# Products on halves of the TensorE array queued side by side in fours and eights, with the mixer's task order set anew

## The chip, the core and the metric

The kernel runs on one core of a Trainium2 chip. The metric is the device time of one execution in microseconds (us). TensorE (PE in the profile) multiplies, with its weight loads shown apart as PEld; VectorE (DVE), ScalarE (ACT) and GpSimd (POOL) do elementwise work, and DMAs are issued mostly from SyncE's queue (SP), a few from ScalarE's.

## The reference, cut to what matters

One decoder layer on 512 tokens with D = 1024, in float32: a feed-forward block, a mixer, a second feed-forward block, each with norms and a residual. The mixer adds three branches: native sparse attention (compressed, selected and window branches), a gated delta rule, and cross-attention into 256 memory tokens. The two parts that the change touches most are the compression of keys and values and the products of values with probabilities:

```python
def compress_blocks(kv, pos_emb, w1, w2):       # for k and for v
    blocks = jnp.concatenate([ch[:, j:j + n_cmp] for j in range(r)], axis=2) + pos_emb[:, None, :]
    flat = blocks.transpose(0, 1, 3, 2, 4).reshape(b, n_cmp, g, CMP_BLOCK * dh)
    return jax.nn.silu(flat @ w1) @ w2          # w1: 2048 x 256

# selected and window branch: 8 heads in 2 groups of 4, head dimension 64
logits = jnp.einsum('bqgjd,bkgd->bgjqk', qb, kb) * NSA_HEAD_DIM ** -0.5 + bias
p = masked_softmax(logits, mask)
return jnp.einsum('bgjqk,bkgd->bqgjd', p.astype(vb.dtype), vb)
```

## The kernel before, in words

Float32 products are made of three products of high and low parts (`mm3`: high by high at L117, low by high or high by low at L118 and L119). A weight tile of 128 x 512 is loaded by SyncE into `wraw` (a ring of 4 buffers), ScalarE copies its high part `whi` (L106), and VectorE, or for some tasks GpSimd, makes its low part `wlo` (L109); each feeds 12 products. The program runs in stages: norm and FFN1, the mixer's projections with the delta rule, attention with the merge of the branches, the output projection, FFN2.

Within a stage the order of work is set by lists of task names in the table `PRM` (`order` for the projections and the delta rule, `order2` for attention and merge, `order0` and `order3` for the stages around them). A scheduler takes the instructions in that order; `off` gives a task a priority that lets its instructions go ahead of earlier tasks, and `pool` says which share of a task's low parts GpSimd makes. Each engine then runs its own list strictly in order. The tasks that the text names:

- `c` is a convolution of the delta rule (`dn_conv`): 24 products into one PSUM bank, then VectorE makes `cacc` from that bank (L217 and three steps at L635), after which the bank can be written again. `z` is the projection to the output gate (`ptm`, 96 products of 512 columns), `M10` a merge tile with products in `pfm`.
- `b0`, `b1` (`dn_subst`) invert 16 x 16 blocks for heads 0 and 1, and 2 and 3: VectorE's substitution (L742, L744) ends in a copy (L745), the result goes to DRAM (`dD`, by ScalarE's queue) and comes back as `Dc` (L749, by SyncE's queue). `e0`, `e1` (`dn_double`, L762) expand `Dc` by a mask into `Dm` and `DT`: three of the four on VectorE, one on GpSimd. The levels `d` (`pt`, L784) then need `Dm`.
- `p0` to `p7` (`cmp_hid`) are the chunks of the compression. A chunk has 4 products of 64 weight columns on 256 columns: two `k` for the keys in the left half of the array's columns (output partitions 0 to 63) and for the values in the right half (64 to 127), all into one bank `phid`. Their weights are two 256 KB tiles `w1` from the ring `wraw`. Being plain float32, a product shows as 2 records.
- `S` (`nsa_soft`) makes scores (`ps`, L1042) and probabilities `Pm`, `P` (`nsa_pt`) their 10 transposes (`ppt`, L1062) and copies to `PT` (L1065: the first two of a tile by VectorE, the third by ScalarE), `V` (`nsa_pv`) the products of values and `PT` (`po`, L1074). There are 8 tasks `V`, one for each pair of heads and branch; each has 8 products with 64 weight columns, over 512, 384, 256 and 128 columns, for group 0 on the left half and for group 1 on the right half of the array. `A` is cross-attention's softmax (`pms` L1083, `pmt` L1097).

Of the kernel before, what the change touches and what calls it, by code (L numbers as in the profile page):

```python
# [10 lines left out]
F32 = mybir.dt.float32  # L11
# [6 lines left out]
P = 128  # L18
# [18 lines left out]
PRM = {'order': ['i', 'a', 'w', 'c01', 'h01', 'r0', 'c00', 'c10', 'c02', 'l0', 'h00', 'h02', 'c12', 'k0', 'h10', 'c22', 'c11', 'h12', 'h11', 'h22', 'r1', 'k1', 'l1', 'b0', 'c21', 'z', 'h21', 'e0', 'c20', 'r2', 'h20', 'c32', 'l2', 'c31', 'd00', 'h31', 'k2', 'r3', 'd01', 'l3', 'b1', 'd02', 'x0', 's00', 'e1', 'd10', 'c30', 'h32', 'x1', 'd11', 'h30', 's01', 's02', 's03', 'q0', 'q3', 'p0', 'o0', 'p1', 'p2', 'p3', 'k3', 'd12', 's10', 'p4', 'q1', 'p5', 's11', 'p6', 'p7', 's12', 's13', 'o1', 'q2', 'f'], 'dma': {'l': 'sync', 'b': 'sync', 'd': 'scalar', 'c': 'sync', 'r': 'sync'}, 'off': {'b0': 300, 'h31': 400, 'r1': 50, 'h32': 50, 'h11': 200, 'h12': 200, 'd10': 100, 'A01': 100, 'A10': 100, 'A11': 100, 'A20': 400, 'A31': 100, 'A21': 20, 'x0': 20, 'x1': 20, 'L': 200, 'S310': 400, 'S001': 20, 'S311': 400, 'A30': 100, 'r0': 400, 'd02': 20, 's11': 100, 'V20': 400, 'l3': 100, 'q1': 20, 'f': 400, 'l1': 20, 'h20': 100, 'h22': 100, 'r3': 50, 'P010': 50, 'y': 100, 'h02': 50, 'S101': 20, 'A00': 100, 'Q0': 50, 'Q1': 200, 'Q2': 50, 'Q3': 50, 'P110': 400, 'V31': 50, 'd01': 200, 'o0': 400, 'p0': 50, 'p1': 50, 'p2': 50, 'p4': 50, 'p5': 20, 'p6': 50, 'p7': 50, 'b1': 200, 'h01': 100, 'M15': 20, 'P201': 400, 'e0': 100, 'e1': 100, 'o1': 20, 'q0': 50, 'q2': 20, 'h21': 20, 'd11': 50, 'p3': 50, 'U0': 100, 's13': 50, 'c11': 20, 's00': 200, 'P011': 400, 'M14': 200, 'c20': 50, 'k2': 20, 'M03': 20}, 'ph': 'e', 'po': 'ss', 'xpd': (0, 1, 2), 'order2': ['K1', 'K0', 'B', 'M10', 'Q0', 'C0', 'Q1', 'S000', 'C3', 'S001', 'P001', 'P000', 'C1', 'S010', 'C2', 'S011', 'V00', 'P010', 'Q2', 'S101', 'S100', 'P011', 'S110', 'V01', 'P100', 'W0', 'P101', 'S111', 'Q3', 'V10', 'P110', 'M12', 'S200', 'P111', 'V11', 'P200', 'S210', 'M14', 'S201', 'M15', 'P201', 'S211', 'W1', 'V20', 'P211', 'P210', 'V21', 'S301', 'S300', 'W2', 'P301', 'S311', 'M11', 'P300', 'L', 'M13', 'S310', 'G0', 'V30', 'P310', 'M16', 'G2', 'P311', 'M17', 'V31', 'W3', 'A00', 'M00', 'A01', 'G1', 'U0', 'M05', 'A10', 'A11', 'G3', 'A30', 'U1', 'A31', 'U3', 'M03', 'M06', 'A20', 'A21', 'U2', 'M07', 'M22', 'M20', 'M02', 'M24', 'M27', 'M21', 'M23', 'M01', 'M04', 'M26', 'M25'], 'order0': ['d0', 'p0', 'n0', 't0', 'd1', 'k2', 'k0', 'p2', 'p3', 'v', 'k3', 'n1', 'k1', 't1'], 'order3': ['s3', 's7', 's2', 's6', 's1', 's5', 's0', 's4', 'd00', 'd01', 'd11', 'g', 'p0', 'n0', 't0', 'd10', 'p1', 'n1'], 't3': (('mm', 'r'), ('e', 's')), 'pool': {'W2': 2, 's13': 3, 'k0': 0, 'k1': 0, 'k2': 0, 'k3': 2, 'p3': 1, 'C0': 1, 'C1': 0, 'C2': 0, 'C3': 2, 'S310': 0, 'L': 3, 'd11': 3, 'p0': 1, 'p1': 1, 'p2': 1, 'p4': 2, 'p5': 1, 'p6': 1, 'p7': 1, 'S311': 0, 'h01': 0, 'h00': 2, 'h02': 0, 'h10': 0, 'h11': 0, 'h12': 0, 'h22': 0, 'h21': 0, 'h20': 0, 'h31': 0, 'h30': 3, 'h32': 0, 'i': 2, 'P011': 2, 'c21': 0, 'd01': 2, 'S000': 0, 'S001': 0, 'S010': 0, 'S011': 0, 'S100': 0, 'S101': 0, 'S110': 0, 'S111': 0, 'S200': 0, 'S201': 0, 'S210': 0, 'S211': 0, 'S300': 0, 'S301': 0, 'M24': 2, 'G2': 2, 'A01': 0, 'M10': 1, 'M15': 2, 'M12': 2, 'M14': 2, 'M13': 2, 'M17': 2, 'M11': 2, 'M16': 2, 'M23': 0, 'M27': 3, 'M01': 2, 'M00': 2, 'M03': 0, 'M07': 2, 'M06': 1, 'M22': 2, 'M04': 2, 'M20': 2, 'M26': 3, 'M02': 0, 'M21': 2, 'M25': 2, 'M05': 2, 'c11': 1, 'o1': 3, 'P000': 2, 'P001': 1, 'P010': 2, 'P100': 2, 'P101': 2, 'P110': 2, 'P111': 2, 'P200': 2, 'P201': 2, 'P210': 2, 'P211': 2, 'P301': 0, 'P300': 2, 'P310': 2, 'P311': 2, 'c12': 0, 'b1': 1, 'x0': 0, 'x1': 0, 'V21': 0, 'c30': 0, 'c01': 0, 'c02': 0, 'c00': 0, 'c10': 0, 'c22': 0, 'c20': 0, 'c31': 0, 'c32': 0, 's01': 3, 'A31': 0, 'd12': 0, 'y': 2, 'G0': 2, 'G1': 2, 'G3': 0, 'U3': 0, 'W3': 2, 'r1': 2, 's12': 3, 'U2': 0, 'Q0': 2, 'Q1': 2, 'Q2': 2, 'Q3': 1, 's00': 3, 's02': 2, 's03': 3, 's10': 2, 's11': 3, 'e1': 2, 'd00': 1, 'U0': 0, 'U1': 0, 'l2': 0, 'd02': 2, 'K1': 3, 'V11': 0, 'V00': 2}, 'pool3': {'d00': 3, 'd01': 3, 'd10': 3, 'd11': 0, 'p1': 2, 't1': 3, 't0': 3, 's5': 2, 's7': 2, 's1': 2, 's0': 2, 's3': 2, 's6': 2, 's2': 2, 's4': 2, 'q0': 1}, 'pool0': {}, 'off0': {'p3': 20, 'n1': 50, 'd0': 200, 'k2': 400, 'k1': 400}, 'off3': {'s1': 20, 's5': 200, 'g': 200, 't0': 400, 'd10': 200, 'p0': 200}, 'tt': ('e', 's'), 'order_s': ['t00', 'w10', 'w00', 'y', 't01', 't02', 'w01', 't03', 'w11', 'R0', 'F000', 'x', 'F101', 'n', 'F200', 't10', 't11', 't12', 't13', 'c', 'F110', 'B', 'F211', 'F011'], 't0': ('e', 's'), 'rs': ((0, 0), (0, 0)), 'ra': (1, 1), 'warm': 8, 'pools': {'F000': 0, 'F101': 0, 'F200': 0, 'F011': 0, 'F110': 0, 'F211': 0, 'w10': 0, 'w11': 0, 't00': 0, 't01': 0, 't02': 0, 't03': 0, 't13': 0, 't10': 0, 't11': 0, 't12': 0, 'w00': 0, 'w01': 0}, 'ptc': 'vvs', 'cva': 'v', 'offs': {'t13': 100, 'R1': 400, 't03': 20, 'w10': 200}, 'vnc': 's', 'sp3': 0, 'hsc': 'vv', 'sf2': 2, 'psc': 'vvvv', 'sp1': 0, 'vbs': 'v', 't1c': 'vs', 'sgv': 256}  # L37


class Body:  # L40
# [172 lines left out]
    def scale(self, eng, out, src, r):  # L213
        if eng == "s":
            self.nc.scalar.activation(out, src, AF.Copy, scale=r)
        else:
            (self.nc.gpsimd if eng == "g" else self.nc.vector).tensor_scalar(out, src, r, None, op0=OP.mult)  # L217
# [709 lines left out]
    def cmp_hid(self, c, Xs, d):  # L927
# [4 lines left out]
        w1 = []  # L932
        for which in range(2):
            w = self.wp.tile([P, 2, 256], F32, tag="wraw", name="w1", bufs=self.WB[0])
            nc.sync.dma_start(w, self.a["cmp_w1"][which, c])
            w1.append(w)
        for k in range(2):
            m = 2 * c + k
            for which in range(2):
                nc.tensor.matmul(d["ph"][64 * which : 64 * which + 64], Xs[which][:, m].rearrange("p g c -> p (g c)"),  # L940
                                 w1[which][:, k], start=m == 0, stop=m == 15)
# [574 lines left out]
```

## Time and profile before

| what | value |
|---|---|
| median of 3 runs | 1361.38 us (1360.89 to 1362.07) |
| the profiled execution | 1360.6 us |
| its span, first to last instruction | 1358.8 us |
| PE busy | 1330.2 us, 98% |
| DVE, ACT, POOL busy | 899.9, 717.7, 142.3 us |
| mean granted TensorE clock | 0.995 |
| DMA | 178.32 MB, mean 131 GB/s |

All times of rows are in us from the span's start, of this one execution. A row of the timeline begins with the start, then the time from its first start to its last end, the engine, the line, the operation and the tiles; xN is the number of records in the row. A span of consecutive matmuls ends a little after the next row starts, since matmuls are pipelined.

### The profile page before, as it was taken

How to read it: one execution, taken by the hardware profiler on the slowest of the kernel's cores; microseconds unless marked ns; L12 is line 12 of the kernel's file. 1: busy time of each engine (PE TensorE's matmuls, PEld its weight loads, DVE VectorE, ACT ScalarE, POOL GpSimd, SP SyncE). 2: the span in 40 equal slices, each digit the busy share in tenths (PEclk: the TensorE clock that was granted, in tenths of full speed). 3: DMA queues.
4: the chain of work that ended last, by engine and by line, in shares of the span. 5: the costliest groups of instructions: out<-in, count | busy, mean ns of one | idle time of the engine just before them, and what ended most of it. 6: DMA issues, size and time to landing. Idle time of an engine off the chain costs nothing.

```text
span 1358.8 us, 21802 instructions
## 1 busy us (share of the span) xinstructions
PE 1330.2 (98%) x7839; PEld 1128.1 (83%) x7839; DVE 899.9 (66%) x1802; ACT 717.7 (53%) x1538; POOL 142.3 (10%) x129
## 2 busy tenths in 40 slices
PE   8999999999999989999999999999999999999997
PEld 7889999788797778787767777788878899998886
DVE  6897876765768775745887323322688778766775
ACT  6566664765655543316655234333576566646652
POOL 0020000000011322003111112323200000000000
PEclk8999999999999999999999999999999999999999
DMA  7543331586664341423111222533744433317773
GB/s 246 194 149 118 100 119 32 178 255 184 210 187 131 83 124 41 126 95 120 52 47 48 78 62 68 189 95 92 257 139 140 135 122 98 121 33 255 199 223 106
DMA packets 107453, 178.32 MB, mean 131 GB/s; under 512 B 18908, under 2 KB 28496, under 8 KB 107344
## 3 DMA queue, kind: packets, MB, share of 16 engines
q1 hardware_dynamic: 107056, 176.67, 41.9%
q8 instruction: 61, 1.00, 0.3%
q14 instruction: 48, 0.39, 0.1%
q10 hardware_dynamic: 288, 0.26, 0.1%
HBM read 166.84 MB, written 10.01 MB: 130 GB/s over the span
## 4 chain that ended last, share of the span: by engine, by line
PE 88%; DVE 5%; ACT 2%; DMA 2%; issue 1%; POOL 0%; SPq 0%; ACTq 0%; DVEq 0%; POOLq 0%
PE smm L429 10%; PE pfm L117 7%; PE pfm L118 7%; PE pfm L119 7%; PE se L429 7%; PE ss L429 3%; PE po L1074 2%; PE ps L1042 2%; PE acc_e L118 2%; PE acc_e L119 2%; PE acc_e L117 2%; PE sr L429 2%; PE acc_s L119 1%; PE acc_s L117 1%; PE acc_s L118 1%; PE so L429 1%
## 5 line engine op out<-in xcount | busy, mean ns | idle before, releaser
L106 ACT CAST whi<-wraw 128x512 fp32r<-128x512 f32 (+1 forms) x314 | 189.8, 614 | 181.4 <-PE pfm L119 65.1
L109 DVE TENSOR_TENSOR wlo<-wraw,whi 128x512 fp32r<-128x512 f32 (+1 forms) x268 | 183.9, 694 | 125.3 <-ACT whi L106 118.2
L117 PE MATMUL pfm<-xth,whi 128*128 128x512 f32 x384 | 154.5, 405 | 3.0 <-DVE cacc L635 3.0
L118 PE MATMUL pfm<-xth,wlo 128*128 128x512 f32 x384 | 154.2, 405 | 1.0 <-POOL wlo L109 1.0
L119 PE MATMUL pfm<-xtl,whi 128*128 128x512 f32 x384 | 154.5, 405 | 0.0
L117 PEld LDWEIGHTS pfm<-xth,whi 128*128 128x128 f32 x384 | 72.4, 189 | 21.0 <-issue 5.2
L119 PEld LDWEIGHTS pfm<-xtl,whi 128*128 128x128 f32 x384 | 72.4, 188 | 16.3 <-issue 2.0
L118 PEld LDWEIGHTS pfm<-xth,wlo 128*128 128x128 f32 x384 | 72.5, 189 | 16.1 <-POOL wlo L109 1.3
L109 POOL TENSOR_TENSOR wlo<-wraw,whi 128x512 fp32r<-128x512 f32 (+1 forms) x43 | 53.6, 1248 | 221.4 <-ACT whi L106 195.2
L106 ACT CAST ringh<-ringr 128x512 fp32r<-128x512 f32 x82 | 50.1, 620 | 42.8 <-PE acc_e L118 8.4
L429 PE MATMUL smm<-thi,fset 128*128 128x256 f32 x384 | 69.4, 279 | 0.0
L109 DVE TENSOR_TENSOR wlo<-ringr,ringh 128x512 fp32r<-128x512 f32 x75 | 51.3, 689 | 21.2 <-PE acc_e L119 6.8
L429 PEld LDWEIGHTS smm<-thi,fset 128*128 128x128 f32 x384 | 58.5, 188 | 0.2
L445 DVE TENSOR_TENSOR up<-smm,s 128x256 f32<-128x256 f32 x32 | 13.6, 424 | 66.5 <-ACT se L442 66.5
L429 PE MATMUL smm<-thi,fxtl 128*128 128x256 f32 x192 | 53.5, 279 | 0.6 <-DVE fxtl L411 0.6
L429 PE MATMUL smm<-thi,fxth 128*128 128x256 f32 x192 | 53.3, 277 | 0.0
L429 PE MATMUL se<-thi,fset 128*128 128x256 f32 x256 | 46.7, 280 | 0.0
L1045 ACT ACTIVATE Pm<-Pm,nm 128x128 f32<-128x128 f32 (+1 forms) x64 | 35.7, 559 | 15.5 <-DVE nm L1044 14.6
L402 DVE TENSOR_TENSOR fs<-fq 128x1024 f32<-128x1024 f32 x32 | 39.0, 1217 | 0.3 <-DMA fq<-in_ffn_u_dram 0.3
L429 PEld LDWEIGHTS se<-thi,fset 128*128 128x128 f32 x256 | 39.1, 187 | 0.0
L123 DVE TENSOR_TENSOR Hl<-H,Hh 128x256 fp32r<-128x256 f32 x88 | 34.9, 420 | 5.6 <-ACT Hh L122 3.7
L1044 DVE CUSTOM_DVE_ANT_0 Pm<-ps,tbl 128x128 f32<-128x128 f32 (+1 forms) x64 | 29.7, 484 | 10.9 <-PE ps L1042 10.3
(565 smaller groups left out, 3946.5 us busy)
## 6 DMA issues: line engine op xcount, KB each, us to landing
wraw<-in_ffn_d_dram SPq DMA_DIRECT2D x94, 256.0 KB, 2.8
ringr<-in_ffn_d_dram SPq DMA_DIRECT2D x82, 256.0 KB, 3.0
fq<-in_ffn_g_dram SPq DMA_DIRECT2D x64, 256.0 KB, 2.8
fq<-in_ffn_u_dram SPq DMA_DIRECT2D x64, 256.0 KB, 2.6
wraw<-in_w_gate_dram SPq DMA_DIRECT2D x48, 256.0 KB, 2.7
wraw<-in_ffn_u_dram SPq DMA_DIRECT2D x34, 256.0 KB, 3.2
wraw<-in_ffn_g_dram SPq DMA_DIRECT2D x34, 256.0 KB, 2.9
woraw<-in_w_out_dram SPq DMA_DIRECT2D x32, 256.0 KB, 3.0
```

What stands on the lines that cost most here:

```text
L106: nc.scalar.copy(hi, raw)
L109: eng.tensor_tensor(lo, raw, hi.bitcast(F32), op=OP.subtract)
L117: t.matmul(out, lh, rh, start=first, stop=False)
L118: t.matmul(out, ll, rh, start=False, stop=False)
L119: t.matmul(out, lh, rl, start=False, stop=last)
L123: return self.nc.vector.tensor_tensor(lo, src, hi.bitcast(F32), op=OP.subtract)
L402: add = lambda *x: v.tensor_tensor(*x, op=OP.add)
L429: m = lambda x, y, **kw: te.matmul(out, x, y, skip_group_check=True, **kw)
L1042: te.matmul(s[:, : max(n, 256)], A[:, qb * P : qb * P + P], K[j][:, : max(n, 256)], start=j == 0, stop=j == 1)
L1044: v.tensor_tensor_reduce(pm, s[:, :n], tb[:, SEQ - n :], -1.0, 3e38, op0=OP.add, op1=OP.min, accum_out=nm[:, qb : qb + 1])
L1045: nc.scalar.activation(pm, pm, AF.Exp, bias=nm[:, qb : qb + 1], scale=-1.0, accum_out=sm[:, qb : qb + 1])
L1074: te.matmul(po[64 * g : 64 * g + 64, kb * P :], vt[:, kb, br * P + 64 * g : br * P + 64 * g + 64], pts[g][:, col[kb] : col[kb] + n], start ...
```

## The change

Three things are done. **First**, a chunk of the compression takes its weights in one DMA: the host lays `cmp_w1` out so that both halves of a chunk are one 512 KB tile, in two buffers of its own in place of the shared ring.

```diff
@@ cmp_hid
-        w1 = []
-        for which in range(2):
-            w = self.wp.tile([P, 2, 256], F32, tag="wraw", name="w1", bufs=self.WB[0])
-            nc.sync.dma_start(w, self.a["cmp_w1"][which, c])
-            w1.append(w)
+        w1 = d["cm"].tile([P, 2, 2, 256], F32, tag="w1", name="w1", bufs=2)
+        nc.sync.dma_start(w1, self.a["cmp_w1"][c])
...
                 nc.tensor.matmul(d["ph"][64 * which : 64 * which + 64], Xs[which][:, m].rearrange("p g c -> p (g c)"),
-                                 w1[which][:, k], start=m == 0, stop=m == 15)
+                                 w1[:, k, which], start=m == 0, stop=m == 15)
```

**Second**, `nsa_soft` returns its last scaling and `nsa_pt` its last copy, and two edges are added to the scheduler (`order`, which only sets places in a list and adds no semaphore): the first transpose of a tile stands behind the last scaling of its `Pm`, and the first product of a task `V` behind the last copies of both its `PT` tiles.

```diff
@@ nsa_pt
-                    te.transpose(pt[:, o : o + P], Pm[:, self.OFF[qb] + kb * P : self.OFF[qb] + kb * P + P], self.ident)
+                    q = te.transpose(pt[:, o : o + P], Pm[:, self.OFF[qb] + kb * P : self.OFF[qb] + kb * P + P], self.ident)
+                    if not bank and not o and PRM.get("gp", 1):
+                        self.order(q, after)
@@ nsa_pv
-                te.matmul(po[64 * g : 64 * g + 64, kb * P :], vt[:, kb, br * P + 64 * g : br * P + 64 * g + 64],
-                          pts[g][:, col[kb] : col[kb] + n], start=br == 0 and kb == 0, stop=False, skip_group_check=True)
+                q = te.matmul(po[64 * g : 64 * g + 64, kb * P :], vt[:, kb, br * P + 64 * g : br * P + 64 * g + 64],
+                              pts[g][0][:, col[kb] : col[kb] + n], start=br == 0 and kb == 0, stop=False, skip_group_check=True)
+                if not kb and not g and PRM.get("gv", 1):
+                    for p in pts:
+                        self.order(q, p[1])
```

**Third**, the tables of `PRM` are set anew. In `order`, `z` goes behind `e0`:

```diff
-'k1', 'l1', 'b0', 'c21', 'z', 'h21', 'e0', 'c20', 'r2', 'h20', 'c32', 'l2',
+'k1', 'l1', 'c21', 'h21', 'b0', 'e0', 'z', 'c20', 'r2', 'h20', 'c32', 'k2', 'l2',
```

Tasks `V` and `p1` to `p7` mostly get the priority 400 where they had 20 to 50 or none, some tasks of `order2`, `order3` and `order0` change places, and low parts move between VectorE and GpSimd for a few tasks (`M10`: all on GpSimd before, all on VectorE now). The number and kinds of TensorE's instructions stay the same.

In TensorE's list, the place of the last task `V` (`V31`; `ppt` are transposes of probabilities, `pms` and `pmt` belong to cross-attention) reads before:

```order
L1074 MATMUL po<-PT,big 64x512
L1062 MATMUL ppt<-cst,Pm 128x128 [waits DVE_49]
L1083 MATMUL pms<-mkT,mq 128x256
L1097 MATMUL pmt<-cst,Pm_8355 128x128 [waits DVE_49]
L1097 MATMUL pmt<-cst,Pm_8355 128x128 x3
L1062 MATMUL ppt<-cst,Pm 128x128
L1074 MATMUL po<-PT,big 64x512
L1083 MATMUL pms<-mkT,mq 128x256
L1074 MATMUL po<-PT,big 64x384 x2
L1074 MATMUL po<-PT,big 64x256
L1074 MATMUL po<-PT,big 64x256 [waits Activation_49]
L1074 MATMUL po<-PT,big 64x128 x2
```

and now:

```order
L117 MATMUL pfm<-xth,whi 128x512
L118 MATMUL pfm<-xth,wlo 128x512
L1101 MATMUL pmt<-cst,Pm_8339 128x128 [waits DVE_49]
L1101 MATMUL pmt<-cst,Pm_8339 128x128 x3
L119 MATMUL pfm<-xtl,whi 128x512
L1075 MATMUL po<-PT,big 64x512 x2
L1075 MATMUL po<-PT,big 64x384 x2
L1075 MATMUL po<-PT,big 64x256 [waits Activation_49]
L1075 MATMUL po<-PT,big 64x256
L1075 MATMUL po<-PT,big 64x128 x2
```

The 8 products stood in three pieces and stand in one row, behind transposes and three products of a projection.

In the same list, where the first chunks of the compression stand (`ptk` are transposes of the delta rule's queries, `pod` and `pst` its outputs and states, `pfm` projections), before:

```order
L678 MATMUL ptk<-cst,qs 128x128 [waits DVE_49]
L678 MATMUL ptk<-cst,qs 128x128 x3
L940 MATMUL phid<-w_6361,X_5944 64x256 [waits DMAHW3_49]
L940 MATMUL phid<-w_6363,X_6110 64x256 [waits DMAHW4_49]
L940 MATMUL phid<-w_6361,X_5944 64x256
L829 MATMUL pod<-S,qdT 128x128
L940 MATMUL phid<-w_6363,X_6110 64x256
L940 MATMUL phid<-w_6416,X_5944 64x256 [waits DMAHW5_49]
L940 MATMUL phid<-w_6418,X_6110 64x256 [waits DMAHW6_49]
L940 MATMUL phid<-w_6416,X_5944 64x256
L940 MATMUL phid<-w_6418,X_6110 64x256
L830 MATMUL pod<-vn,QK 128x128
```

and now:

```order
L678 MATMUL ptk<-cst,qs 128x128 [waits DVE_49]
L678 MATMUL ptk<-cst,qs 128x128 x3
L937 MATMUL phid<-w_6323,X_5944 64x256
L937 MATMUL phid<-w_6323,X_6110 64x256
L937 MATMUL phid<-w_6323,X_5944 64x256
L937 MATMUL phid<-w_6323,X_6110 64x256
L937 MATMUL phid<-w_6402,X_5944 64x256
L937 MATMUL phid<-w_6402,X_6110 64x256
L937 MATMUL phid<-w_6402,X_5944 64x256
L937 MATMUL phid<-w_6402,X_6110 64x256
L117 MATMUL pfm<-xth,whi 128x512
```

The products of two chunks stood in pieces of 3 and 5 with `pod` in between, and now the 8 stand together right behind `ptk`; the later chunks stand in fours.

In VectorE's list, from the copy that ends the substitution of `b0` (L745) to the first steps of the next convolution's `cacc`, before:

```order
L745 COPY Bi<-Bi 64x256 [waits DVE_49]
...
L139 SCALAR_TENSOR_TENSOR dry<-drz,dry 128x4 [waits DVE_49]
L109 TENSOR_TENSOR wlo<-wraw,whi 128x512 [waits DMAHW7_49,PE_49,Activation_49]
L671 TENSOR_TENSOR kn<-ptr_5507,dry 128x512 [waits DVE_49,Pool_49]
L109 TENSOR_TENSOR wlo<-wraw,whi 128x512 [waits DMAHW0_49,Activation_49]
L762 TENSOR_TENSOR Dm<-Dc,msk 128x512 [waits DMAHW4_49]
L762 TENSOR_TENSOR Dm<-Dc,msk 128x512
L762 TENSOR_TENSOR DT<-Dc,msk 128x512
L217 TENSOR_SCALAR cacc<-pfm,cw 128x512 [waits PE_49]
L109 TENSOR_TENSOR wlo<-wraw,whi 128x512 [waits DMAHW1_49,Activation_49]
L635 SCALAR_TENSOR_TENSOR cacc<-pfm,cw,cacc 128x509 [waits DVE_49]
L635 SCALAR_TENSOR_TENSOR cacc<-pfm,cw,cacc 128x510 [waits DVE_49]
```

and now:

```order
L745 COPY Bi<-Bi 64x256 [waits DVE_49]
L109 TENSOR_TENSOR wlo<-wraw,whi 128x512 [waits DMAHW7_49,PE_49,Activation_49]
L109 TENSOR_TENSOR wlo<-wraw,whi 128x512 [waits DMAHW0_49,PE_49,Activation_49]
L762 TENSOR_TENSOR Dm<-Dc,msk 128x512 [waits DMAHW6_49]
L762 TENSOR_TENSOR Dm<-Dc,msk 128x512
L762 TENSOR_TENSOR DT<-Dc,msk 128x512
L109 TENSOR_TENSOR wlo<-wraw,whi 128x512 [waits DMAHW1_49,PE_49,Activation_49]
L109 TENSOR_TENSOR wlo<-wraw,whi 128x512 [waits DMAHW3_49,Activation_49]
L217 TENSOR_SCALAR cacc<-pfm,cw 128x512 [waits PE_49]
L109 TENSOR_TENSOR wlo<-wraw,whi 128x512 [waits DMAHW5_49,Activation_49]
L635 SCALAR_TENSOR_TENSOR cacc<-pfm,cw,cacc 128x509 [waits DVE_49]
L635 SCALAR_TENSOR_TENSOR cacc<-pfm,cw,cacc 128x510 [waits DVE_49]
```

The small steps of a norm (L129 to L139) and the scaling L671 have left the place ahead of the expansions, and the two low parts behind them now stand ahead of `cacc`.

## Rows read from the trace of the kernel before

**Rows 1.** Page, part 1: busy us (share) and records of each engine.

```profile
PE 1330.2 (98%) x7839; PEld 1128.1 (83%) x7839; DVE 899.9 (66%) x1802; ACT 717.7 (53%) x1538; POOL 142.3 (10%) x129
```

**Rows 2.** Windows: stretch, busy us of PE, PEld, DVE, ACT, POOL; clock; DMA.

```profile
420.00:640.00 220.00, 211.00 (x1201) 169.56 (x1200) 145.14 (x376) 97.80 (x228) 46.50 (x47) 1.00 0.34 96
640.00:800.00 160.00, 160.00 (x821) 115.65 (x820) 102.33 (x320) 77.55 (x210) 24.41 (x19) 1.00 0.20 63
```

**Rows 3.** TensorE's waits: for what, us in total, times, longest.

```profile
PE pfm L117 <- DVE cacc L635: 3.0, 1, 3.0
PE pfm L118 <- POOL wlo L109: 1.0, 1, 1.0
```

**Rows 4.** TensorE's timeline: eight products in a row, and what follows.

```profile
720.58 2.37 PE L1074 MATMUL po<-PT,big 128*64 128x512 f32 x16
722.89 0.55 PE L1062 MATMUL ppt<-cst,Pm 128*128 128x128 f32 x3
```

**Rows 5.** TensorE's timeline: a lone product, and four transposes elsewhere.

```profile
776.78 0.60 PE L1062 MATMUL ppt<-cst,Pm 128*128 128x128 f32 x4
777.31 1.07 PE L1074 MATMUL po<-PT,big 128*64 128x512 f32 x2
...
778.91 0.60 PE L1097 MATMUL pmt<-cst,Pm 128*128 128x128 f32 x4
779.35 0.27 PE L1062 MATMUL ppt<-cst,Pm 128*128 128x128 f32 x1
```

**Rows 6.** Window of attention, line L1074 alone: all its records.

```profile
655.00:785.00 130.00, 25.61 (x128) 9.67 (x128) 1.00 0.18 55
```

**Rows 7.** Line L1074 by form: weight loads, ns min/median/max.

```profile
L1074 PEld LDWEIGHTS po<-PT,big x128: 132/137/137, 661.1 to 782.3; 128*64 128x64 f32 x128
```

**Rows 8.** TensorE's timeline: compression's products in fives, ones and twos.

```profile
564.43 1.51 PE L940 MATMUL phid<-w,X 128*64 128x256 f32 x10
...
567.70 0.65 PE L940 MATMUL phid<-w,X 128*64 128x256 f32 x2
...
589.90 0.65 PE L940 MATMUL phid<-w,X 128*64 128x256 f32 x4
```

**Rows 9.** Window of the compression, line L940 alone: all its records.

```profile
560.00:603.00 43.00, 13.14 (x64) 5.13 (x64) 1.00 0.44 129
```

**Rows 10.** VectorE's timeline around the expansions of e0, then e1.

```profile
492.99 0.37 DVE L745 COPY Bi<-Bi 64x256 f32<-64x256 f32 x1
...
499.19 3.01 DVE L762 TENSOR_TENSOR Dm<-Dc,msk 128x512 f32<-128x512 f32 x2
...
503.82 0.74 DVE L217 TENSOR_SCALAR cacc<-pfm,cw 128x512 f32<-128x512 f32 x1
...
565.30 0.37 DVE L745 COPY Bi<-Bi 64x256 f32<-64x256 f32 x1
...
573.21 0.69 DVE L762 TENSOR_TENSOR Dm<-Dc,msk 128x512 f32<-128x512 f32 x1 [5.98 <-DMA Dc<-dD]
```

**Rows 11.** TensorE's timeline: the two products behind the one that waited 3.0.

```profile
508.31 0.39 PE L118 MATMUL pfm<-xth,wlo 128*128 128x512 f32 x1
508.54 0.40 PE L119 MATMUL pfm<-xtl,whi 128*128 128x512 f32 x1
```

**Rows 12.** TensorE's timeline: two transposes and products of values behind them.

```profile
726.66 0.38 PE L1062 MATMUL ppt<-cst,Pm 128*128 128x128 f32 x2
...
726.97 2.27 PE L1074 MATMUL po<-PT,big 128*64 128x512 f32 x14
```

**Rows 13.** DMA issues: engine, count, KB each, median us to landing.

```profile
dx<-xa SPq DMA_DIRECT2D x4, 512.0 KB, 2.8
...
rowsb<-drows SPq DMA_DIRECT2D x4, 512.0 KB, 5.6
```

**Rows 14.** TensorE's timeline: the queries' transposes, and e1's first level.

```profile
562.48 0.60 PE L678 MATMUL ptk<-cst,qs 128*128 128x128 f32 x4
...
580.54 0.56 PE L784 MATMUL pt<-Dm,LT 128*128 128x64 f32 x4
```

## What the change should do to the time, predicted before it ran

> **What bounds the kernel now.** I began with the page's busy times: TensorE is busy for 1330.2 of the 1358.8 us of the span, VectorE for two thirds of it [rows 1]. Next come the windows of the two stages that the change touches: TensorE works for 211.0 of 220 us among the delta rule's projections and for 160.0 of 160 in attention, at the full granted clock (1.00, which is 2.4 GHz) in both [rows 2]. So TensorE's own list is the bound. Time can leave in two ways only: its work gets shorter, or one of its waits goes. The waits in these stages are few; the largest are 3.0 us for `cacc` (a convolution's bank is not yet read by VectorE) and 1.0 us for a low part that GpSimd makes [rows 3]. The list of TensorE holds the same instructions after the change as before, so what the work can lose is decided by how two neighbours share the array. That I looked up in the timeline.
>
> **Values times probabilities.** Where the 8 products of a task `V` stand together, they take from 720.58 to the next row's start at 722.89, 2.31 us, though the row is drawn 2.37 long: the drawn end lies 0.06 behind the next start [rows 4]. A product of 512 columns alone takes 1.07 − 0.06 = 1.0 us [rows 5]. The 8 have 2 × (512 + 384 + 256 + 128) = 2560 columns; one after the other they would take 5.0 us at the lone product's rate, so in the row each left half runs beside a right half. Passing from full-width work into such a row also costs something: four transposes take 0.53 us ahead of a lone product (776.78 to 777.31) and 0.44 elsewhere (778.91 to 779.35), so 0.09 for each piece [rows 5].
>
> Now: the timeline shows the 64 products in 19 pieces, with 25.61 us drawn [rows 6]. Less 19 × 0.06 that is 24.5 us. After: 8 rows of 2.31, 18.5 us. Saved: 6.0, and 11 entries fewer, 1.0. **7.0 us** in all. This is work on TensorE with no wait in that stage [rows 2], so it counts in full.
>
> At this place a rule of the notes speaks against the change. The rows first: the run of 16 records contains its 16 weight loads, of 137 ns each in the middle [rows 7], 2.2 us in sum, and still takes 2.31 with all products [rows 4]. The Trainium skill, page "TensorE: Matmul & The Clock Gate", section "Part 3: Packing small matmuls — row/col tiling", says that a weight load overlaps with running products only when its row group differs; both halves here use the same rows, all 128. By it every load would stand in the open and a row would cost about 4.5 us. The trace does not agree with it, and the sum goes by the row; what the rule would give stands below as a rival.
>
> **The compression.** A lone product and two side by side are both drawn 0.65 us long, five are drawn 1.51 [rows 8]: five are three pairs' worth, so each further pair adds (1.51 − 0.65) / 2 = 0.43. The 32 products stand in 15 pieces with 13.14 us drawn [rows 9], less 15 × 0.06 it is 12.2. After: one row of 8, 0.65 + 3 × 0.43 − 0.06 = 1.88, and six rows of 4 at 0.65 + 0.43 − 0.06 = 1.02, together 8.0. Saved: 4.2, and 8 entries fewer, 0.7: **5.0 us**, rounded.
>
> So TensorE's work falls by 12.0 us. What remains is what the waits become; the sum of four places:
>
> **The expansions of `e0`.** VectorE stands in order at the first `Dm` until `Dc` is back. Before, `Dc` was there when VectorE came, 5.8 us after the end of the copy L745 (493.36 to 499.19), so the trip takes at most 5.8; at `e1` it took 7.5 (565.67 to 573.21) with VectorE idle [rows 10]. Behind it stand 4.6 us of expansions (to 503.82), `cacc`, and with it the bank that TensorE waited for until about 508.0 [rows 10, 11]. The change puts the next convolution's two low parts ahead of `cacc`, behind the expansions, and takes the small norm steps away. The first of them then ends 5.8 to 7.5 + 4.6 + 0.7 (a step of that size, [rows 10]) = 11.1 to 12.8 us after the copy. What TensorE has till then: three low parts (the ring) that are made, 12 products each at 0.23 us [rows 11], 8.3 us, and up to 2.8 of a tile begun: 8.3 to 11.1. A wait of 0 to 4.5 in place of 3.0; with one tile's cover less it would be 7.3, and below zero it can't be. I take 2.0, near the middle: **1.0 less**, between 3.0 less and 4.3 more.
>
> **GpSimd's low part.** `M10`'s low parts go to VectorE, which is busy 102 of 160 us there [rows 2]: the 1.0 of [rows 3] goes, **1.0 less** (0 if VectorE is as late).
>
> **Copies ahead of the rows of eight.** Seven of the eight rows now begin 0.2 to 0.4 us of work behind the last transposes of their tile, and the third pair needs a tile that ScalarE still has to copy, about half of a 0.74 step of 512 columns [rows 10]. Before, a row began at 726.97 right behind two transposes (726.66, 0.38 long) and ran 14 records in 2.27 us, as fast as the row of [rows 4], [rows 12]. Between 0 and 8 × 0.37 = 3.0; nearer to that row: **0.8 more**.
>
> **New weight tiles and `e1`.** The first two chunks' weights are loaded far ahead, the third's load waits for the first chunk's products. 512 KB land in 2.8 us in the quicker row and 5.6 in the slower one [rows 13]; by the new list there are about 3.9 us of work between that release and the products that need it, so 0 to 1.7 for the third chunk, and as a rule less for the later ones. On SyncE's queue `Dc` of `e1` stands behind the load of the fourth. From the queries' transposes to `e1`'s first level there were 18.1 us [rows 14]; the new list has 8.8 (4 + 8 transposes, 8 and twice 4 products of the compression, 13 of a projection, by the prices above). VectorE's copy stands three small steps behind the scaling that these transposes wait for, 0.8, then 7.5 of trip and 0.7 of expansion: 9.0. So 0.2, and more if `Dc` is held up: 0 to 3 for both, **1.2 more**.
>
> The rest of the tables (`order3`, `order0`, other low parts) moves work between places where TensorE never waited for it; I set it at nothing, covered by TensorE's full list, ± 1.
>
> **Sum.** −12.0 − 1.0 − 1.0 + 0.8 + 1.2 = −12.0, from the profiled execution's 1360.6: 1348.6. The median of the runs lies 0.8 above that execution, so 1349.4.
>
> **Rivals.** (1) *The waits go as well.* If z's products cover the round trip (its low parts stand in the substitution now), and the other places cost nothing: −12.0 − 3.0 − 1.0 = −16.0, 1345.4. For it: TensorE gets z's 96 products of cover between; against it: VectorE had idle time only at `e1`. (2) *New waits take the place.* e0's wait at 7.3, copies 3.0, weights and `e1` 3.0: −12.0 + 4.3 − 1.0 + 3.0 + 3.0 = −2.7, 1358.7; at two thirds of that, 1355.6. For it: the compression's weights come in two buffers of 512 KB where four of 256 KB stood, and nothing in the trace shows how that runs. (3) *Slower: the round trip of `Dc` bare at both places.* With the ring empty when VectorE stands at `Dm`, TensorE waits for the trip, the expansions and a low part, 12.8 us, at `e0`, and 9.0 at `e1`: −12.0 − 3.0 − 1.0 + 12.8 + 9.0 = +5.8, 1367.2. It decides for slower once the two exceed 16.0 + 2.7 = 18.7 us together. Against it: before, VectorE's 6.0 us of idleness at `e1` cost TensorE nothing [rows 10, 3]. (4) *The rows do not pair* and every weight load is in the open: 8 × (4.5 − 24.5 / 8) = +11.5 for the values; 1372.9. [Rows 4] speaks against it.
>
> **How the numbers follow.** A measurement of this kernel tells about 0.2%, 2.7 us, from no change. Chances: forecast 0.50 (1346.5 to 1353), rival 1 0.18, rival 2 0.24, rival 3 0.06, rival 4 0.02. Rival 2 is faster for two thirds of its chance, the rest within 0.2%; so faster 0.84, same 0.08, slower 0.08. The range leaves out the lower end of rival 1, the upper third of rival 2 and the slower cases: 1344 to 1357.
>
> **What would show it.** Right: line L1075 in eight rows of 16 records at 2.3 us, some 19 us drawn; L937 in seven rows, some 8.4; TensorE's busy time near 1318; the wait for GpSimd gone. Wrong: a row of eight broken by a wait for `PT`; waits for `w1` above 3 us; TensorE idle behind L762 for more than 5 us at either place; or rows whose records start one after another.

## The result, and the profile after

The changed kernel takes 1347.04 us in the median (1346.16 to 1348.22, 4 runs) against 1361.14 (1359.14 to 1362.07, 4 runs): 0.9899 of the time, 95% interval 0.9882 to 0.9916. That is 14.1 us less, where 12.0 less was forecast (1349.4, range 1344 to 1357).

The profiled execution of after has a span of 1344.4 us, 14.4 less than before. Its page's first part, as in [rows 1]:

```profile
PE 1317.5 (98%) x7839; PEld 1126.1 (84%) x7839; DVE 903.7 (67%) x1804; ACT 713.4 (53%) x1536; POOL 140.5 (10%) x127
```

TensorE works 12.7 us less with the same number of records; its idle time falls from 28.6 to 26.9. Where the time left is read from the first starts of four kinds of products in the trace:

| stretch (from, to the first start of) | before | after | difference | forecast |
|---|---|---|---|---|
| start, first convolution product | 411.2 | 409.8 | −1.4 | 0 |
| from there, first score product `ps` | 233.6 | 228.6 | −5.0 | −5.8 |
| from there, first product of the output projection | 308.4 | 300.7 | −7.7 | −6.2 |
| from there, end | 405.6 | 405.3 | −0.3 | 0 |

The forecast's column sorts its terms by place: the compression, `M10`, `e0` and the weight tiles lie in the second stretch, the values and their copies in the third.

The windows of line L1075 (as in [rows 6]) and L937 (as in [rows 9]) of after, columns as in [rows 2] with PE and PEld alone:

```profile
655.00:785.00 130.00, 19.00 (x128) 8.51 (x128) 1.00 0.20 61
...
545.00:603.00 58.00, 8.45 (x64) 3.97 (x64) 1.00 0.35 103
```

19.00 us in place of 25.61, and 8.45 in place of 13.14. Three of the rows themselves, from TensorE's timeline of after:

```profile
563.61 1.95 PE L937 MATMUL phid<-w,X 128*64 128x256 f32 x16
...
568.76 1.08 PE L937 MATMUL phid<-w,X 128*64 128x256 f32 x8 [0.23 <-DMA w<-in_cmp_w_dram]
...
655.50 2.38 PE L1075 MATMUL po<-PT,big 128*64 128x512 f32 x16
```

Eight products of values are drawn 2.38 us long, as in [rows 4] (2.37). Of the compression, eight are drawn 1.95 us long and four 1.08; the prediction had 1.94 and 1.08. And TensorE's waits in after, over the whole span, the view of [rows 3]:

```profile
PE ptk L678 <- DVE qs L671: 2.7, 2, 1.6
...
PE ptk L678 <- DVE Bi L744: 1.8, 1, 1.8
PE ptk L678 <- DVE kn L671: 1.7, 1, 1.7
...
PE pfm L117 <- ACT whi L106: 1.0, 1, 1.0
...
PE pkk L722 <- POOL kbT L700: 0.6, 1, 0.6
...
PE phid L937 <- DMA w<-in_cmp_w_dram: 0.4, 2, 0.2
...
PE pfm L117 <- DVE cacc L635: 0.3, 1, 0.3
```

The 3.0 us for `cacc` have become 0.3. The wait for GpSimd's low part is gone too, but the 1.0 that this view puts to ScalarE's `whi` stands in its place, at the same tile of `M10` (more of it below). The transposes `ptk` now wait 6.2 us in four places. Before, the same view of the projections had 2.1 for them:

```profile
PE ptk L678 <- DVE kn L671: 2.1, 2, 1.7
```

### The profile page after: what moved, and what is told of

Its sections match the earlier page's. It is cut to its first block, busy times and chain, and to the rows that moved or that the text cites. A ratio compares the mean times of both kernels' runs of the same rounds, so it can differ in the third digit from the quotient of the medians.

```text
span 1344.4 us, 21791 instructions
## 1 busy us (share of the span) xinstructions
PE 1317.5 (98%) x7839; PEld 1126.1 (84%) x7839; DVE 903.7 (67%) x1804; ACT 713.4 (53%) x1536; POOL 140.5 (10%) x127
## 4 chain that ended last, share of the span: by engine, by line
PE 88%; DVE 5%; DMA 3%; ACT 2%; issue 1%; SPq 0%; POOL 0%; DVEq 0%; ACTq 0%
PE smm L429 10%; PE pfm L117 7%; PE pfm L119 7%; PE pfm L118 7%; PE se L429 7%; PE ss L429 3%; PE acc_s L119 2%; PE acc_s L117 2%; PE acc_s L118 2%; PE ps L1039 2%; PE sr L429 2%; PE so L429 1%; PE acc_e L118 1%; PE acc_e L119 1%; PE acc_mm L117 1%; PE acc_e L117 1%
## 5 line engine op out<-in xcount | busy, mean ns | idle before, releaser
L109 DVE TENSOR_TENSOR wlo<-wraw,whi 128x512 fp32r<-128x512 f32 x270 | 188.2, 705 | 108.1 <-ACT whi L106 102.3
L429 PEld LDWEIGHTS smm<-thi,fxtl 128*128 128x128 f32 x192 | 36.0, 188 | 1.0 <-DVE fxtl L411 1.0
```

What stands on the lines that cost most here:

```text
L109: eng.tensor_tensor(lo, raw, hi.bitcast(F32), op=OP.subtract)
L429: m = lambda x, y, **kw: te.matmul(out, x, y, skip_group_check=True, **kw)
```

## The experiments

Twelve kernels were run. The theory was the prediction's: what counts is TensorE's work, and that follows from the pieces in which half-width products stand in its list. The price of a piece in the expectations is that of the prediction, written by columns: the longer of its two halves' columns at 1.67 ns, plus 0.15 (that gives 1.0 us for a lone 512 and 2.29 for a row of eight), plus 0.09 for entering. The main rival was that the new tables, by shorter waits, made the gain. All medians are in this table; "drawn" is the time of the lines' records in the profiled execution, as in [rows 6] and [rows 9] (for the compression of no_w1 and old_order partly at the lower granted clock, of which more below). The kernel before, run again beside them, had medians of 1360.8, 1360.4 and 1360.6.

| kernel | pieces, values / compression | drawn, us | median (range), us |
|---|---|---|---|
| before | 19 / 15 | 25.6 / 13.1 | 1361.1 (1359.1 to 1362.1) |
| changed | 8 / 7 | 19.0 / 8.5 | 1347.0 (1346.2 to 1348.2) |
| no_edges | 19 / 7 | 26.1 / 8.5 | 1355.9 (1354.9 to 1358.0) |
| no_w1 | 8 / 13 | 19.0 / 13.2 | 1352.5 (1352.0 to 1354.4) |
| code_only | 15 / 13 | 23.1 / 11.0 | 1363.0 (1361.0 to 1369.4) |
| tables_only | 19 / 13 | 26.2 / 12.3 | 1361.0 (1360.0 to 1362.4) |
| halves_apart | 8 / 7 | 31.4 / 8.5 | 1358.5 (1356.0 to 1359.7) |
| code_prio | 12 / 9 | 21.4 / 9.3 | 1358.7 (1356.6 to 1362.3) |
| old_order | 8 / 9 | 19.0 / 12.5 | 1351.6 (1349.5 to 1368.1) |
| m10_pool | 8 / 7 | as changed | 1346.0 (one run) |
| pv_only | 14 / 15 | 22.8 / 13.1 | 1359.8 (1358.0 to 1360.6) |
| w1_only | 20 / 13 | 25.8 / 11.0 | 1366.5 (1362.2 to 1370.0) |
| old_order2 | 9 / 7 | 19.2 / 8.5 | 1348.1 (1347.0 to 1349.2) |
| late_transposes | 8 / 7 | 19.0 / 8.5 | 1343.9 (1342.7 to 1345.1) |

### Undoing one part: the edges, the weight tile

The edges are left out of the changed kernel (no_edges):

```diff
-                    if not bank and not o and PRM.get("gp", 1):
+                    if not bank and not o and PRM.get("gp", 0):
...
-                if not kb and not g and PRM.get("gv", 1):
+                if not kb and not g and PRM.get("gv", 0):
```

> The changed kernel without the two scheduling edges of nsa_pt and nsa_pv; tables and weight tiles as changed. TensorE's list then has the 64 products of values in 19 pieces (1, 4, 3, 1, 7, 5, 3, 1, 4, 3, 1, 7, 4, 4, 1, 2, 5, 4, 4 products) in place of eight eights. Theory (the gain is TensorE's work, and a piece costs the longer of its two halves' columns at 1.67 ns plus 0.15, plus 0.09 for the entry): 26.3 us in place of 19.0, so +7.3 to about 1354.3, and L1075 drawn about 26 us long. Rival (the gain came from the tables, by shorter waits): within 2 us of the changed kernel, below 1349.

Measured: 1355.9, 8.9 above the changed kernel; L1074 is drawn 26.1 us long. The theory holds and the rival falls. The stage is 9.7 us longer (310.4): 8.2 of it is TensorE's work, the rest idle time, of which this view of TensorE's waits names the two largest parts (`pct` are the transposes of the compressed branch's probabilities).

```profile
PE ppt L1060 <- DVE Pm L216: 0.8, 1, 0.8
PE pct L994 <- DVE cs L991: 0.7, 1, 0.7
```

The two edges were taken out together; what each is worth alone was not tried.

The weight tile is taken back to two tiles of the ring (no_w1), the diff of the change read backwards:

```diff
-        w1 = d["cm"].tile([P, 2, 2, 256], F32, tag="w1", name="w1", bufs=2)
-        nc.sync.dma_start(w1, self.a["cmp_w1"][c])
+        w1 = []
+        for which in range(2):
+            w = self.wp.tile([P, 2, 256], F32, tag="wraw", name="w1", bufs=self.WB[0])
...
```

> The changed kernel with the compression's weights loaded as before, in two 256 KB tiles of the shared ring. TensorE's list then has the compression's products in 13 pieces (one of 8, then six times 1 and 3) in place of one of 8 and six of 4. Theory (work by pieces): 12.6 us in place of 8.6, +4.0 to about 1351.0. Rival (the single products hide in waits for the weights' DMAs, which stand at the same place): less than 1.5 us, below 1348.5.

Measured: 1352.5, 5.5 above the changed kernel. In the profiled execution, at 1354.4 the longest of its four, the projections take 235.9 us, 7.3 more: about 4 of work as expected, a wait of 1.7 for a weight tile, and behind that wait something that the expectation didn't have. Two windows of no_w1, columns as in [rows 2], the third number from the end the granted clock:

```profile
560.00:570.00 10.00, 7.90 (x52) 5.50 (x50) 5.45 (x24) 5.64 (x22) 1.29 (x1) 1.00 0.54 130
570.00:580.00 10.00, 10.00 (x45) 5.32 (x46) 5.49 (x14) 1.88 (x3) 1.05 (x1) 0.83 0.50 158
```

Behind the wait (it ended at 569.33) the granted clock was at its lower level, 1.2 GHz, for part of the window: 0.83 of 10 us costs 1.7.

### One part alone: code without tables, tables without code

code_only has the change's code with the old tables, tables_only the old code with the changed tables; each is one kernel's text with the other's line `PRM = {...}`.

```diff
-PRM = {'order': [..., 'k1', 'l1', 'c21', 'h21', 'b0', 'e0', 'z', 'c20', ...
+PRM = {'order': [..., 'k1', 'l1', 'b0', 'c21', 'z', 'h21', 'e0', 'c20', ...
```

> The code of the change (edges, weight tile) with the old tables. The list has the products of values in 15 pieces (the last five are eights), the compression's in 13 pieces. Theory (work by pieces): 34.5 us against 39.4 before and 27.6 after, so 4.9 below the kernel before, about 1356.2, waits of 3.0 and 1.0 us as before. Rival (the edges alone make the gain): 1349 or below. Rival (the tables make it): within 1.5 us of the kernel before.

> The code of the kernel before with the changed tables. 19 pieces of values, 13 of the compression. Theory (work by pieces): 38.9 against 39.4 us, so 0.5 less, and the changed waits (3.0 for the convolution's bank and 1.0 for GpSimd's low part gone, some 3 us of new ones for transposes) about 1 less: 1359 to 1361. Rival (the tables make the gain): below 1353.

Measured: 1361.0 for the tables alone, the time before, as expected. 1363.0 for the code alone: 2.2 slower than the kernel before beside it (ratio 1.0025, 1.0009 to 1.0041), where 4.9 less was expected; all three expectations missed, the last of them by 0.7. Its pieces were as expected (23.1 and 11.0 drawn), so the work did fall; the time came back as waits and as a lower clock. From TensorE's waits in code_only:

```profile
PE pfm L117 <- DVE cacc L635: 3.0, 1, 3.0
PE phid L937 <- DMA w<-in_cmp_w_dram: 2.3, 1, 2.3
...
PE pfm L118 <- POOL wlo L109: 1.6, 2, 1.0
...
PE ppt L1061 <- DVE Pm L217: 1.1, 2, 0.9
```

and from windows of one us, behind the first of them:

```profile
505.00:506.00 1.00, 0.00 (x0) 0.00 (x0) 1.00 (x2) 0.00 (x0) 0.00 (x0) 1.00 0.44 130
506.00:507.00 1.00, 0.66 (x3) 0.56 (x4) 0.96 (x3) 0.77 (x2) 0.00 (x0) 0.92 0.93 128
507.00:508.00 1.00, 1.00 (x6) 0.80 (x5) 1.00 (x2) 0.37 (x1) 0.00 (x0) 0.50 0.87 306
508.00:509.00 1.00, 1.00 (x4) 0.87 (x4) 0.89 (x2) 0.53 (x3) 0.00 (x0) 0.50 0.35 135
509.00:510.00 1.00, 1.00 (x4) 0.75 (x3) 0.00 (x0) 0.94 (x6) 0.00 (x0) 0.50 0.47 156
510.00:511.00 1.00, 1.00 (x5) 0.81 (x4) 0.90 (x3) 0.01 (x1) 0.00 (x0) 0.87 0.28 107
```

TensorE stood for 3.0 us, went on at 506.34, and from about 506.9 to 510.3 its granted clock was at 1.2 GHz, half: some 1.7 us more for a wait that the kernel before had as well, in its profiled execution without that price.

To part the two edits, each was put alone into the kernel before (pv_only: the edges; w1_only: the weight tile; the diffs are those above):

> The kernel before with nothing but the two scheduling edges of nsa_pt and nsa_pv. Values in 14 pieces (1, 2, 5, 1, 2, 2, 3, 1, 7, then five eights), compression in 15 as before. Work by pieces alone: 36.5 us against 39.4, 2.9 less, 1358. Theory now (the edges under the old order make TensorE wait for scalings and copies, as in the run of the code with the old tables): gain given back by waits of 1 to 3 us ahead of transposes, 1359 to 1361. Rival (the new weight tile alone spoiled that run): 1358 or below, without waits in attention.

> The kernel before with nothing but the compression's weights in one 512 KB tile with two buffers. Values in 20 pieces, compression in 13. Work by pieces alone: 37.4 us against 39.4, 2.0 less, 1359. Theory now: a wait of 2 to 3 us for a weight tile comes in (two buffers, and loads queued behind others on SyncE's queue), with the clock at half for some 3 us behind it in some executions: 1360 to 1363. Rival (the edges alone spoiled that run): 1359 or below.

Measured: pv_only 1359.8 as expected (ratio to before 0.9996, 0.9987 to 1.0006): of 2.9 us of work less, 0.8 arrives, which is not clear of noise. w1_only 1366.5, 5.9 above before and 3.5 beyond the expectation's upper end. Its waits in the projections:

```profile
PE pfm L116 <- DVE cacc L634: 3.0, 1, 3.0
PE phid L936 <- DMA w<-in_cmp_w_dram: 2.6, 2, 2.3
```

So the weight tile is what made code_only slow: its products wait 2.6 us for weights (2.3 in code_only) where the kernel before waited 0.3. That the old order brings them too soon for two buffers is the reading of these waits; more buffers were not tried. The ten runs of w1_only fit a clock that falls behind such waits by differing amounts: the three lowest, 1362.2 to 1363.6, had mean clocks of 0.997, 0.994 and 0.997, the five above 1366.9 of 0.992 to 0.994; 0.001 of 1360 us is 1.4 us. The fit is rough (0.997 also stands beside 1364.9), and that the clock made this spread is argued from these means; no trace of one of the longer runs shows it.

### Which tables matter

code_prio adds to code_only nothing but the changed priorities of `V` and `p`:

```diff
+'V00': 400, 'V01': 400, 'V10': 400, 'V11': 400, 'V21': 400, 'V30': 400, 'V31': 400,
+'p1': 400, 'p2': 400, 'p3': 400, 'p4': 400, 'p5': 400, 'p6': 400, 'p7': 400,
```

> The code of the change with the old tables, but with the changed priorities of the tasks V and p. The list has the values in 12 pieces (8, 8, 5, 1, 1, 1, 8, 8, 8, 1, 7, 8) and the compression in 9 (8, 4, 4, 4, 1, 2, 1, 4, 4). Theory (work by pieces): 30.9 us against 39.4 before, with the cheaper exits 9 less, and the waits of the old order stay (3.0 for the convolution's bank, after which the clock may fall, and 1.0): 1351 to 1354. Rival (the reordering of the other tasks is what lets the code gain, since the code with the old tables gained nothing): above 1357.

Measured: 1358.7. The rival's number, though the work was as expected (21.4 and 9.3 drawn): the code and the priorities make most of the long rows, and what is left of the old tables gives the work back. Its waits are 3.6 us for the compression's weights (0.3 before), 3.0 for `cacc` (as before) and 1.6 for GpSimd's low parts (1.0 before), and the clock falls behind the second.

old_order and old_order2 are the changed kernel with one old list each:

```diff
-'order': ['i', 'a', 'w', ..., 'c21', 'h21', 'b0', 'e0', 'z', 'c20', ...]
+'order': ['i', 'a', 'w', ..., 'b0', 'c21', 'z', 'h21', 'e0', 'c20', ...]
```

> The changed kernel with the old list 'order' (projections and delta rule: z ahead of e0 again), everything else as changed. Values stay in eight eights, the compression has 9 pieces. Theory: 0.9 us more work; the wait of 3.0 for the convolution's bank comes back in place of 0.3, and the waits of transposes for queries and keys fall from 6.2 to about 2: about 0 from the waits, up to 1.7 more where the clock falls after the wait: 1347.5 to 1350. Rival (z's place behind e0 is worth its 2.7 in full): 1351 or above.

> The changed kernel with the old list 'order2' (attention and merge), everything else as changed. Values in 9 pieces (six eights, 2, 6, 8). Theory: 0.3 us more work, and waits ahead of transposes come back where products of values stood between them: 1 to 4 us more, 1348 to 1351. Rival (the order of attention's tasks is worth nothing once the edges and priorities stand): below 1348.

Measured: 1351.6 with the old `order`, 4.5 above the changed kernel, on the rival's side; 1348.1 with the old `order2`, 1.1 above, at the lower edge of its expectation and 0.1 from its rival. So of these two lists that of the projections counts for more; that of attention counts for little once edges and priorities stand. The profiled execution of old_order is no picture of its median (it took 1368.1); it is used below for the clock alone.

For m10_pool, `M10`'s low parts go back to GpSimd (`'M10': 0` to `'M10': 1`):

> The changed kernel with M10's low parts on GpSimd again; TensorE's list is the same. Theory: the one wait of about 1.0 us for GpSimd's low part comes back at M10 and nothing else changes (time within 1.5 us). Rival: the changed order hides it, no wait at M10.

Measured: one run, 1346.0, 0.1 below the changed kernel's shortest. The wait returns:

```profile
PE pfm L117 <- POOL wlo L108: 1.0, 1, 1.0
```

Yet nothing is lost, for the changed kernel waits at the same tile one product earlier; the view of m10_pool has no such wait for `whi`. TensorE's timeline of after, then of m10_pool:

```profile
629.83 0.47 PE L117 MATMUL pfm<-xth,whi 128*128 128x512 f32 x1 [1.04 <-ACT whi L106]
```

```profile
627.92 0.47 PE L116 MATMUL pfm<-xth,whi 128*128 128x512 f32 x1
629.40 0.50 PE L117 MATMUL pfm<-xth,wlo 128*128 128x512 f32 x1 [1.02 <-POOL wlo L108]
```

VectorE's timeline of after shows what it did just ahead of that wait's end:

```profile
625.72 2.53 DVE L109 TENSOR_TENSOR wlo<-wraw,whi 128x512 fp32r<-128x512 f32 x2
628.28 1.40 DVE L1012 TENSOR_TENSOR KL<-pfm,KH 64x512 fp32r<-64x512 f32 x2
```

The two low parts now stand ahead of `KL`, VectorE's reading of a bank of `pfm`, which ends at 629.68, 0.15 before the product starts. In m10_pool `KL` starts at 626.37, the same product at 627.92 without a wait, and that step `whi` only at 628.47, so the product cannot need it: by these rows it was `KL` that ended the wait. From the products `pcl` ahead of this tile to the first score product it takes 10.68 us before (634.10 to 644.78), 10.61 after (627.79 to 638.40) and 10.69 in m10_pool (627.07 to 637.76): the place of `M10`'s low parts is worth 0.1 us at most.

### What makes a row of eight short

halves_apart keeps the eight together but lets the halves follow each other:

```diff
-        for kb in range(TB):
-            n = SEQ - kb * P
-            for g in range(2):
+        for g in range(2):
+            for kb in range(TB):
+                n = SEQ - kb * P
```

> The changed kernel with the two loops of nsa_pv exchanged: the four products of group 0 (left half of the array's columns) first, then the four of group 1 (right half), still eight in a row. Theory (a row is short because a left and a right product of the same size run at once, neighbours in the list): the four of one half have 1280 columns, 2.13 us at 1.67 ns, so a row takes some 4.4 us, of which one overlap at the change of halves is lost or kept: 4.0 to 4.4 in place of 2.31, +13 to +17 in all, 1360 to 1364. Rival (any eight in a row are quick, since only the entries count): 2.3 us each and 1347.

Measured: 1358.5, 11.4 above the changed kernel, a little under the theory's range and far from the rival. A row of TensorE's timeline:

```profile
668.93 3.93 PE L1075 MATMUL po<-PT,big 128*64 128x512 f32 x16
```

3.93 us drawn in place of 2.38, 8 × 1.55 = 12.4: the neighbours must be a left and a right half. Only where the left half's last products meet the right half's first does some of it overlap.

### A version beyond both

What the changed kernel has left in the projections are mostly the waits of `ptk`. late_transposes emits three of these groups one task later and ties them behind a product of that task:

```diff
+        def late(after=None):
             p = psb("e", "ptk")
             for i in range(TB):
-                te.transpose(p[:, i], n[:, i], self.ident)
+                q = te.transpose(p[:, i], n[:, i], self.ident)
+                if after is not None and not i:
+                    self.order(q, after)
             nc.scalar.copy(T, p)
...
+'order': [..., 'c02', 'j01', ..., 'c22', 'j10', ..., 'z', 'j21', ...]
```

> The changed kernel, with three of the delta rule's groups of transposes (ptk of keys of head 0, of queries of head 1, of keys of head 2) emitted one task later and tied behind the 11th, 10th and 59th product of the task that runs there, some 8 products (1.9 us) later in TensorE's list. Theory (what is left of TensorE's idle time in the projections is that it reaches these transposes before VectorE's norm steps are done; waits of 1.7, 1.6 and 1.8 us): up to 5 us less, 1342 to 1344. Rival (the next users of the keys, GpSimd's product and pkk, then come late by the same time): no change, 1346 to 1348.

Measured: 1343.9 (1342.7 to 1345.1), 0.9880 of the kernel before (0.9863 to 0.9896), 3.1 below the changed kernel. The three waits are gone, and of 5.2 us some 2 come back elsewhere, the largest at `zg`, the output gate that ScalarE makes from z's bank; TensorE's waits in the projections of late_transposes:

```profile
PE pfm L117 <- ACT zg L578: 1.7, 1, 1.7
PE ptk L681 <- DVE qs L673: 1.2, 1, 1.2
PE phid L946 <- DMA w<-in_cmp_w_dram: 1.1, 2, 0.7
PE pfm L117 <- ACT whi L105: 1.0, 1, 1.0
PE pfm L118 <- DVE wlo L108: 0.9, 1, 0.9
```

## Why the prediction was right, and where its terms were off

**The bound and the work.** That TensorE's list bounds the kernel, and that pieces price its half-width products, held: 12.7 us less work against 12.0 over the whole span, 5.2 of it in the projections and 7.9 in attention (0.4 more outside). *Values*: the records' part came as reckoned, 25.61 − 19 × 0.06 less 19.00 − 8 × 0.06 = 5.9 against 6.0. The whole stage's work fell by 7.9 (308.29 to 300.41 in the windows between the marks of the table above), so what hangs on the number of pieces is about twice the 1.0 of the entries: transposes take 1.0 and scores 1.3 less in sum from start to start. Whether that is the way out of a row, which the prediction left at nothing, was not separated. *Compression*: 13.14 − 15 × 0.06 less 8.45 − 7 × 0.06 = 4.2, as reckoned. no_edges and no_w1 show both parts in the time.

**`e0`.** The term took 2.0 us of wait in place of 3.0; 0.3 are left. VectorE's timeline of after:

```profile
490.93 0.38 DVE L745 COPY Bi<-Bi 64x256 f32<-64x256 f32 x1
...
498.07 2.16 DVE L762 TENSOR_TENSOR Dm<-Dc,msk 128x512 f32<-128x512 f32 x2 [3.99 <-DMA Dc<-dD]
...
501.95 0.74 DVE L217 TENSOR_SCALAR cacc<-pfm,cw 128x512 f32<-128x512 f32 x1
```

The trip took 6.8 us from the copy's end (491.31 to 498.07), within the bounds of 5.8 and 7.5; VectorE stood idle for 4.0 and TensorE didn't notice, since z's low parts had been made before. The expansions took 2.8 (498.07 to 500.83) where 4.6 were set; GpSimd worked beside them from 498.8 to 503.4 before and only from 498.1 to 499.7 after, but whether that is the reason was not separated. That is rival 1's mechanism at this place, and rival 3's condition, a ring that is empty there, did not come.

**`e1` and the weights.** 1.2 us more were set; 0.4 came, all for the third and fourth chunk, where the kernel before had 0.3, so 0.1 more. At `e1` the reckoning of 9.0 us against 8.8 was close to what happened: `Dm` could start at 571.41,

```profile
571.41 0.69 DVE L762 TENSOR_TENSOR Dm<-Dc,msk 128x512 f32<-128x512 f32 x1 [0.51 <-DMA Dc<-dD]
```

and TensorE's first level started at 572.37, right behind other work: cover to spare there is none.

**The copies ahead of the rows.** 0.8 was set; TensorE's waits in the whole attention stage are 0.2 us, for `pmt`, and none for these copies. The lower bound was the right end.

**`M10`.** 1.0 less was set, 0.1 came. The prediction's condition, 0 if VectorE is as late, is what happened: the low part no longer waits for GpSimd, but on VectorE it delays `KL`, and the wait of 1.02 became one of 1.04 at the product before. The prediction read VectorE's load from the window 640:800, and the wait stood at 636.

**What was not named.** "The rest at nothing" was the step that failed: the order of the `c` and `h` tasks was part of that rest, and with the new list `order` the transposes `ptk` come before VectorE's norm steps are done, four waits with 6.2 us in place of 2.1 (1.7 in old_order, which has the old list). The four named places were forecast to give nothing in sum and gave 2.6 less: 2.7 less at `e0`, 0 at `M10` and the copies, 0.1 more at the weights. `ptk` took 4.1 back and smaller waits gave 1.1, so that TensorE's idle time in the second and third stretch of the table is 0.4 more, where 0 was forecast. That the sum of the waits came out right is luck: errors of 1.7, 0.8, 1.1 and 1.1 on one side, and of 1.0 and 4.1 on the other. The span of the profiled execution fell by 14.4 where 12.0 was forecast; the difference is 1.1 us of work in these two stretches, 0.3 at the end and 1.4 ahead of the first convolution, less those 0.4. Of the 1.4, 0.6 lie before the first product of `smm` (70.4 against 71.0), where TensorE's list is the same in both; there the window 10:20 has a granted clock of 0.75 before and 1.00 after, so that part is one execution against another.

**The rivals.** Rival 4 is out: rows run in 2.38 us drawn, with their weight loads inside. The rule of the Trainium skill, page "TensorE: Matmul & The Clock Gate", section "Part 3: Packing small matmuls — row/col tiling", that loads overlap only with another row group, does not describe these rows. What shortens a row is shown by halves_apart: neighbours on different column halves. Rival 2 is not what the changed kernel did, but it is what parts of the change do alone: pv_only, w1_only, code_only and code_prio all have less work and new waits in its place.

**Parts that don't add.** The prediction costed edges, weight tile and tables as one and gave the tables nothing but their waits. In the runs the code alone loses 2.2, the tables alone gain nothing, and together they gain 14.1. Of the 11.7 between code_prio and the changed kernel, the list `order` holds 4.5 and `order2` 1.1, each taken back alone; the rest, in the interplay of the tables, was not separated. In old_order TensorE waits 3.0 us for `cacc` and 1.2 for weights again, in place of 0.3 and 0.4: the new list puts `z` over the round trip at `e0` and moves the compression's chunks. Which of the two counts for more was not tried.

## What to carry to other kernels

Where TensorE's list is full, look for half-width products that stand alone: a left and a right half as neighbours cost as much as one, and long rows save the entries too. Work saved this way arrives only if what stood between the products is placed where it still covers the waits of the other engines; after such a regrouping read the waits anew, since a table that was right for the old pieces may lose all of the gain. And a short wait can cost its length again, or far more, through the clock, so look at the granted clock behind every wait of 1 to 3 us.

## What the runs showed of the hardware that was not expected

The granted clock fell behind waits of 1 to 3 us, but not behind each. Of the six profiled executions with the wait of 3.0 us for `cacc`, five (code_only, code_prio, pv_only, w1_only, old_order) show 0.91 in the window 500 to 520, some 1.7 us lost in each as in the finer windows above, and the kernel before shows 1.00. In no_w1 one of 1.7, with one of 0.4 some 2 us earlier, was followed by the fall shown above. In m10_pool one of 1.91 for `ptk` was followed by 0.86 and 0.80 in the windows 480:485 and 485:490, 1.7 us lost, while the changed kernel waited 1.84 at the same place and stayed at 1.00. In old_order's profiled execution two waits close together were followed by a long stretch at half; TensorE's timeline and windows there:

```profile
573.46 1.08 PE L936 MATMUL phid<-w,X 128*64 128x256 f32 x8 [1.21 <-DMA w<-in_cmp_w_dram]
...
575.91 0.48 PE L846 MATMUL pot<-cst,on 128*128 128x128 f32 x1 [0.94 <-DVE on L845]
```

```profile
570.00:575.00 5.00, 3.76 (x18) 2.18 (x18) 3.39 (x7) 0.62 (x1) 1.49 (x1) 1.00 0.75 228
575.00:580.00 5.00, 4.09 (x13) 1.73 (x14) 3.14 (x12) 0.69 (x1) 0.00 (x0) 0.58 0.54 157
580.00:590.00 10.00, 10.00 (x41) 7.35 (x41) 1.99 (x5) 0.69 (x1) 0.00 (x0) 0.50 0.17 54
590.00:600.00 10.00, 10.00 (x45) 8.56 (x45) 1.82 (x5) 0.38 (x1) 0.62 (x2) 0.50 0.00 0
600.00:610.00 10.00, 10.00 (x48) 9.68 (x47) 3.07 (x7) 1.10 (x2) 0.00 (x0) 0.50 0.07 26
610.00:620.00 10.00, 10.00 (x64) 7.62 (x64) 2.66 (x8) 0.63 (x3) 0.00 (x0) 0.66 0.02 5
```

From about 576 to 617 TensorE was busy nearly all the time at 1.2 GHz. By these windows 2.1 + 15 + 3.4 = some 20 us were lost, more than the whole change brought; this execution is 16.6 us above the kernel's median. What decides how long it lasts stays open.
